# Two chained transformer blocks in one kernel: the experts' weight splits, the diff attention's order, an inverse's steps and the latent attention's meta keys

## The chip, the cores and the metric

The kernel runs on one core of one Trainium2 chip, as a single launch. The metric is device time in microseconds: the median of three runs. Beside it there is one profiled execution, with a time and a span of its own; every row below comes from that one. Engines are named as the profile names them: PE (TensorE matmuls) and PEld (its loads of the stationary operand), DVE (VectorE), ACT (ScalarE), POOL (GpSimd), SP (SyncE, here an issuer of DMAs).

## The reference

Two blocks run one after the other on x of 1024 tokens by 1024 columns, all in float32. The first has two layers, each of token mixers and an expert-choice FFN; layer 0 also carries 256 context tokens through both. The second is a gated delta rule layer and a latent attention layer. What the change touches:

```python
def diff_attn_core(q, k, v, lam):                    # 4 heads, two maps per head
    s = einsum('bqhmd,bkhmd->bhmqk', q, k) * (DIFF_D ** -0.5)
    a = softmax(s, axis=-1)
    w = a[:, :, 0] - lam * a[:, :, 1]
    return einsum('bhqk,bkhd->bqhd', w, v)

def expert_choice_ffn(x, router_w, wg, wu, wd):      # 16 experts, wg, wu, wd 1024x1024 each
    cap = 2 * n // 16                                # 128 tokens of x, 32 of the context
    aff = softmax(einsum('bnd,de->bne', x, router_w), axis=-1)
    gate, idx = top_k(aff.transpose(0, 2, 1), cap)
    xg = x[bidx, idx]
    hid = silu(einsum('becd,edf->becf', xg, wg)) * einsum('becd,edf->becf', xg, wu)
    o = einsum('becf,efd->becd', hid, wd) * gate[..., None]
    return zeros_like(x).at[bidx, idx].add(o)

def gated_delta_rule(q, k, v, g, beta):              # 8 heads, chunks of 64 tokens
    system = lower + eye(c)                          # lower: strictly lower triangle of kb k^T * decay
    sol = triangular_solve(system, rhs, left_side=True, lower=True)
    ...

def chunk_causal_attention(q, k, v):                 # 8 heads; 16 meta keys ahead of the 1024
    p = softmax(where(mask, q_blk k^T * scale, NEG), -1)
    return einsum('bhqk,bkhd->bqhd', p, v)
```

## The kernel before

The stages run in order: layer 0's mixers (diff attention 392 to 600 us of the span), its experts (about 949 to 1735), layer 1's mixers (diff attention 2055 to 2220), its experts (2505 to 3195), the delta layer (3195 to 4125, its heads 3300 to 3990), the latent layer's inputs, its attention (4490 to 4765) and its output (to the end). Float32 operands of large products are split into a high part (`wh`, written by ACT) and a low part (`wl`, what is left, by a subtraction), and each product is made of three matmuls: high by high, low by high, high by low. The instructions of an engine are put in order by a scheduler at build time that takes program order as the priority; semaphores between engines follow from the tiles.

**Experts.** `experts(l)` makes three products per expert, gate, up and down. `product` takes two halves of a weight; `weight` allots a raw tile of 2 MiB from the three buffers of `self.wr`, loads it on SP's queue, and splits it block by block: ACT copies 128x1024 to `wh` (L1165), DVE subtracts three of the four blocks, POOL the fourth (L1166). `wh` and `wl` have two buffers of four blocks. Each half then has 24 matmuls of 128x512 (L1187), and in layer 0, ahead of them, the context's: 16 matmuls with 32 stationary columns against the raw weight (L1181), which the trace shows as 32 records. `run` puts steps of other work between the yields of a product: the flips (`flip`: four transposes into the bank `t`, ACT's copy, DVE's subtraction L1134) and the hidden products. `fetch` gathers an expert's tokens and `scatter` adds its results, both through POOL (L1220).

**Diff attention.** `diff_unit` is one head by one block of 128 queries: 32 units in layer 1, 40 in layer 0 with the context's own 8. `a(m)` makes the scores of map m (PE, L591), their reduce (DVE, L592) and their exp (ACT, L594). `b` scales the second map by lambda and the ratio of the sums (DVE: reciprocal L598, one column L599, 128x1280 L600) and adds the two maps (POOL, L601). `c` transposes (L615) and copies (L616), `d` multiplies by V. `units` takes them in a pipeline: a(0) of unit k, b of unit k-1, a(1) of unit k, d of units k-3 and k-4, c of unit k-2.

**Inverses.** The triangular systems of a head are inverted by `inverse` for three groups of chunks: the meta tokens (`[8]`, one small chunk), and two groups of four. Each is a generator that yields after each set of small matmuls (64x64, 16 records a set) with an estimate of its cost. `inverses` takes one step of each in turn, and `weave` sets those steps between the matmuls of the next head's front (`zmul`, L1358).

**Latent attention.** `unit` in `latent_attend` is one head by one query block, 64 units. `a` makes scores and exp, `c` transposes the weights in blocks of 128 keys, the meta keys as a block of 16 (L2130), `d` multiplies by V: first the 16 meta rows (L2145), then the blocks (L2147).

Of the kernel before, what the change touches and what calls it, by code (L numbers as in the profile page):

```python
# [23 lines left out]
NE = 16  # L24
# [38 lines left out]
class Kernel:  # L63
# [490 lines left out]
    def units(self, q, new, steps):  # L554

        for i, u in enumerate(new):
            q.append(u)
            k = len(q) - 1
            old = [q[k - x] if k >= x else None for x in range(6)]
            if old[0]:  # L560
                old[0]["a"](0)
            if old[1]:
                old[1]["b"]()
            if old[0]:
                old[0]["a"](1)
            for x in (0, 1):
                if old[3 + x] and old[3 + x]["t"] % 2:
                    old[3 + x]["d"](old[4 + x], x)
            for x in (0, 1):
                if old[2]:  # L570
                    old[2]["c"](x)
            if old[0]:
                self.now = old[0]["sm"][:, 2:3]
            for _ in range(-(-len(steps) // (len(new) - i))):
                steps.pop(0)()

    def diff_unit(self, p, ps, V, Y, h, Z, t):
# [6 lines left out]
        def a(m):  # L584
# [7 lines left out]
            nc.vector.tensor_reduce(U["mx"][:, m:m + 1], S[:, :nk], AX.X, OP.min)  # L592
# [46 lines left out]
    def nbr_unit(self, p, ps, V, Y, h, H, i):  # L639
# [35 lines left out]
        def b():  # L675
# [434 lines left out]
    def experts(self, l):  # L1110
# [5 lines left out]
        with self.pool("ex") as p, self.banks("exps", m=3, c=1, t=1) as ps:  # L1116
# [52 lines left out]
            def product(U, key, x, name, e):  # L1169

                pm = U[key] = ps("m", 2)
                pc = None
                X = U[x]
                for half in range(2):
                    w, *W = weight(name, e, half)
                    if ctx and half == 0:
                        pc = U[key + "c"] = ps("c")
                    for k in range(4 if ctx else 0):
                        b = half * 4 + k
                        for g in range(4):  # L1180
                            nc.tensor.matmul(pc[g * 32:(g + 1) * 32, :256], U[x[0] + "cT"][:, b % 2 * 128 + b // 2 * 32:b % 2 * 128 + b // 2 * 32 + 32],  # L1181
                                             w[:, k, g * 256:(g + 1) * 256], start=b == 0, stop=b == 7)
                        yield
                    for k in range(4):
                        for q, (i, j) in enumerate(((0, 0), (0, 1), (1, 0))):
                            for c in range(2):
                                nc.tensor.matmul(pm[:, c], X[i][:, half * 4 + k], W[j][:, k, c * 512:(c + 1) * 512],  # L1187
                                                 start=half + k + q == 0, stop=half == 1 and k == 3 and q == 2)
# [44 lines left out]
            run(product(E[0], "g", "xT", "exp_w_gate", 0), [], 0)  # L1233
            silu(E[0])
            run(product(E[0], "u", "xT", "exp_w_up", 0), fetch(1), 0)
            for e in range(NE):
                U = E[e]
                steps = hidden(U)
                if e + 1 < NE:
                    run(product(E[e + 1], "g", "xT", "exp_w_gate", e + 1), steps, 1)  # L1240
# [4 lines left out]
                run(product(U, "d", "hT", "exp_w_down", e), [], 0)  # L1245
                scatter(U, e)
                if e + 1 < NE:
                    run(product(E[e + 1], "u", "xT", "exp_w_up", e + 1), fetch(e + 2) if e + 2 < NE else [], 0)
# [837 lines left out]
    def latent_attend(self, pw, p, ps, X):  # L2086
# [3 lines left out]

        def weight(c):
# [6 lines left out]
        def load(h):  # L2098
            H = {"mm": self.latent_head(X, h) if h else self.first}
            H["v"] = p.tile([128, 9, 128], F32, name="v", bufs=2)  # L2100
            hs = slice(h % 2 * 128, (h % 2 + 1) * 128)
            nc.sync.dma_start(H["v"][:, :8], self.vd[h // 2][16:, hs].rearrange("(t p) c -> p t c", p=128))
            nc.sync.dma_start(H["v"][:16, 8], self.vd[h // 2][:16, hs])
# [5 lines left out]
        def unit(H, h, i):  # L2109
# [15 lines left out]
            def c():  # L2125
                e = U["e"]
                eT = U["eT"] = p.tile([128, 9, 128], F32, name="eT", bufs=2)
# [213 lines left out]
```

## Time and profile before

| what | us |
|---|---|
| median of three runs (4869.22 to 4873.66) | 4869.98 |
| the profiled execution's own time | 4872.44 |
| its span | 4870.5 |

The span is what the profile's rows cover; 1.9 us of the profiled execution lie outside it. A window row gives the busy time of each engine in a stretch; the rest of the stretch is idle time of that engine. An engine at the full length of a stretch bounds it; where none is, waits between engines do.

### The profile page before, as it was taken

What the parts mean: (1) busy time and instruction counts of PE and PEld (TensorE: products, weight loads), DVE (VectorE), ACT (ScalarE), POOL (GpSimd) and SP (SyncE); (2) the same over time, 40 slices, a digit from 0 to 9 for tenths busy, and PEclk for the clock granted to TensorE, in tenths of its full rate; (3) what the DMA queues carried; (4) which work ended last, traced back from release to release, by engine and by line L of the source; (5) the groups of instructions that cost most, each with busy time, mean ns of one, the idle gap of its engine ahead of it and who ended that gap; (6) DMA issues with size and microseconds to landing.
All of it is one profiled execution on the core that took longest, in us unless ns stands there. A gap on an engine that the chain in (4) does not pass through costs nothing.

```text
span 4870.5 us, 77258 instructions
## 1 busy us (share of the span) xinstructions
PE 4427.4 (91%) x30151; PEld 3480.5 (71%) x30151; DVE 3183.5 (65%) x6512; ACT 2225.7 (46%) x4037; POOL 1358.2 (28%) x1033
## 2 busy tenths in 40 slices
PE   8998889799999979989959888879999998898899
PEld 4686676476777757867747666658888876787787
DVE  6536877755555566397778998856666663676551
ACT  3326653255555543376336656643333331454330
POOL 2214502244454422162124444412111100022111
PEclk9999899899999989999979999989999999999999
DMA  6422246687878722313548988821111123146757
GB/s 209 159 89 63 60 140 252 217 295 285 291 285 293 279 87 84 103 48 92 202 160 327 329 320 316 309 95 45 36 36 45 41 61 119 56 169 224 191 151 150
DMA packets 333997, 817.14 MB, mean 168 GB/s; under 512 B 32524, under 2 KB 125380, under 8 KB 333632
## 3 DMA queue, kind: packets, MB, share of 16 engines
q1 hardware_dynamic: 228368, 602.22, 34.2%
q0 software_dynamic: 51520, 125.07, 10.9%
q10 hardware_dynamic: 53744, 84.92, 5.0%
q8 instruction: 237, 3.88, 0.3%
q14 instruction: 128, 1.05, 0.1%
HBM read 690.47 MB, written 121.66 MB: 167 GB/s over the span
## 4 chain that ended last, share of the span: by engine, by line
PE 30%; DVE 8%; issue 5%; ACT 4%; DMA 3%; POOL 1%; SPq 0%; ACTq 0%; POOLq 0%; DVEq 0%
PE ps_z L1358 8%; PE ps_m L1187 5%; DVE wl L1166 4%; ACT wh L1165 2%; PE ps_mm L2211 2%; PE ps_S L2119 2%; PE ps_t L2147 1%; PE ps_m L917 1%; PE ps_i L1680 1%; PE ps_i L1694 1%; PE ps_m L1854 1%; PE ps_i L1687 1%; POOL wl L1166 1%; PE ps_t L1482 1%; PE ps_o L1599 1%
## 5 line engine op out<-in xcount | busy, mean ns | idle before, releaser
L1166 DVE TENSOR_TENSOR wl<-w,wh 128x1024 fp32r<-128x1024 f32 x576 | 843.5, 1508 | 179.7 <-ACT wh L1165 179.7
L1165 ACT ACTIVATE wh<-w 128x1024 fp32r<-128x1024 f32 x768 | 754.6, 1050 | 264.0 <-PE ps_m L1187 151.5
L1166 POOL TENSOR_TENSOR wl<-w,wh 128x1024 fp32r<-128x1024 f32 x192 | 535.7, 2825 | 634.9 <-ACT wh L1165 571.1
L1187 PE MATMUL ps_m<-wl,xTh 128*128 128x512 f32 x1024 | 344.6, 411 | 49.0 <-DVE wl L1166 33.6
L1187 PE MATMUL ps_m<-wh,xTh 128*128 128x512 f32 x1024 | 336.2, 410 | 1.4 <-ACT xTh L1133 1.4
L376 PE MATMUL ps_mm<-wh,hh 128*128 128x256 f32 (+1 forms) x928 | 322.5, 350 | 9.3 <-ACT wh L313 6.1
L1187 PE MATMUL ps_m<-wh,xTl 128*128 128x512 f32 x1024 | 325.1, 399 | 0.0
L376 PE MATMUL ps_mm<-wl,hh 128*128 128x256 f32 (+1 forms) x928 | 317.9, 344 | 2.7 <-DVE wl L314 2.6
L376 PE MATMUL ps_mm<-wh,hl 128*128 128x256 f32 (+1 forms) x928 | 316.1, 342 | 0.0
L1358 PE MATMUL ps_z<-hh,wh 128*128 128x350 f32 (+2 forms) x792 | 277.5, 351 | 2.0 <-ACT hh L1291 1.2
L1187 PEld LDWEIGHTS ps_m<-wl,xTh 128*128 128x128 f32 x1024 | 190.0, 192 | 114.4 <-DVE wl L1166 51.9
L1358 PE MATMUL ps_z<-hl,wh 128*128 128x350 f32 (+3 forms) x792 | 268.1, 339 | 0.0
L1358 PE MATMUL ps_z<-hh,wl 128*128 128x350 f32 (+2 forms) x792 | 264.5, 334 | 0.0
L601 POOL TENSOR_TENSOR e<-e,e 128x1280 f32<-128x1280 f32 (+1 forms) x72 | 191.6, 2661 | 188.2 <-DVE e L600 154.8
L1187 PEld LDWEIGHTS ps_m<-wh,xTh 128*128 128x128 f32 x1024 | 188.0, 192 | 64.2 <-issue 14.4
L1187 PEld LDWEIGHTS ps_m<-wh,xTl 128*128 128x128 f32 x1024 | 195.1, 192 | 41.3
L592 DVE TENSOR_REDUCE mx<-ps_S 128x1 f32<-128x1280 f32 (+1 forms) x144 | 196.1, 1366 | 37.0 <-PE ps_S L591 36.3
L376 PEld LDWEIGHTS ps_mm<-wh,hh 128*128 128x128 f32 x928 | 177.3, 192 | 48.0 <-issue 11.0
L376 PEld LDWEIGHTS ps_mm<-wl,hh 128*128 128x128 f32 x928 | 178.5, 192 | 22.4 <-DVE wl L314 4.4
L594 ACT ACTIVATE e<-ps_S,mx 128x1280 f32<-128x1280 f32 (+1 forms) x144 | 177.4, 1233 | 33.2 <-DVE mx L592 22.0
L376 PEld LDWEIGHTS ps_mm<-wh,hl 128*128 128x128 f32 x928 | 177.5, 192 | 18.8 <-issue 0.8
L1187 PE MATMUL ps_m<-wl,hTh 128*128 128x512 f32 x512 | 165.0, 403 | 20.5 <-DVE wl L1166 12.7
(661 smaller groups left out, 10754.0 us busy)
## 6 DMA issues: line engine op xcount, KB each, us to landing
w<-in_exp_w_gate SPq DMA_DIRECT2D x64, 2048.0 KB
w<-in_exp_w_up SPq DMA_DIRECT2D x64, 2048.0 KB
w<-in_exp_w_down SPq DMA_DIRECT2D x64, 2048.0 KB
w<-in_ada_w SPq DMA_DIRECT2D x12, 2048.0 KB
z<-zd POOLq DMA_DIRECT2D x76, 320.0 KB, 4.6
wraw<-in_ada_w SPq DMA_DIRECT2D x38, 512.0 KB
zd<-hi ACTq DMA_DIRECT2D x76, 256.0 KB
zw<-in_t_win SPq DMA_DIRECT2D x64, 256.0 KB
```

The source lines that it names most:

```text
L376: nc.tensor.matmul(pm[:, o:], hs[i][x][:, k, a * 128:(a + 1) * 128], w[:, k % 2, o:], start=q == 0, stop=q == 23)
L592: nc.vector.tensor_reduce(U["mx"][:, m:m + 1], S[:, :nk], AX.X, OP.min)
L594: nc.scalar.activation(e[:, :nk], S[:, :nk], AF.Exp, scale=-1.0, bias=U["mx"][:, m:m + 1], accum_out=U["sm"][:, m:m + 1])
L601: nc.gpsimd.tensor_add(w[:, :nk], w[:, :nk], U[0][:, :nk])
L917: nc.tensor.matmul(pm, a[:, k], b[:, k], start=k + x == 0, stop=k == 7 and x == 2)
L1165: nc.scalar.activation(wh[:, k], w[:, k], AF.Copy)
L1166: (nc.gpsimd if k == 3 else nc.vector).tensor_sub(wl[:, k], w[:, k], wh[:, k].bitcast(F32))
L1187: nc.tensor.matmul(pm[:, c], X[i][:, half * 4 + k], W[j][:, k, c * 512:(c + 1) * 512], start=half + k + q == 0, stop=half == 1 and k == 3 ...
L1358: nc.tensor.matmul(q[:M, :n], a[:, k % 4], b[:, k, z0:z0 + n], start=k == 0 and x == 0, stop=k == 7 and x == 2)
L1482: nc.tensor.transpose(pt[:r, i * 128:(i + 1) * 128], src[:, tok(t0 + i)[1]], self.ident)
L2119: nc.tensor.matmul(S[:, ks], q[:, i * 128:(i + 1) * 128], k[:, ks], start=x == 0, stop=x == 4)
L2211: nc.tensor.matmul(pm[:, c], a[:, k], b[:, k, c * 512:(c + 1) * 512], start=k + z == 0, stop=k == 7 and z == 2)
```

## The change

It has five parts. In `units`, both a(0) and a(1) of unit k come ahead of b of unit k-1, and b's L599 and L600 are put behind the second reduce of unit k on DVE. In `experts`, splitting becomes a queue: pieces of four blocks, one ahead, in layer 0; pieces of two blocks, three ahead, in layer 1, with `ahead + 1` and `ahead + 2` buffers; ACT's copies and the subtractions take two blocks per instruction, and all subtractions are DVE's. In layer 0 the context's matmuls of both halves stand at the start of a product. In layer 1 the context's bank of PSUM becomes a second one for the flips. `inverses` steps its two groups of four together, with one yield, and then the meta group. In `latent_attend` the meta keys are a block of 128: the transpose takes 128 columns, 16 rows are copied into a zeroed tile, and the product has 128 rows, 112 of them zero in both operands.

```diff
@@ units
             if old[0]:
                 old[0]["a"](0)
+                old[0]["a"](1)
             if old[1]:
-                old[1]["b"]()
-            if old[0]:
-                old[0]["a"](1)
+                old[1]["b"](old[0] and old[0].get("max"))
@@ diff_unit
-            nc.vector.tensor_reduce(U["mx"][:, m:m + 1], S[:, :nk], AX.X, OP.min)
+            U["max"] = nc.vector.tensor_reduce(U["mx"][:, m:m + 1], S[:, :nk], AX.X, OP.min).ins
...
-        def b():
+        def b(behind):
             sm, w = U["sm"], U[1]
             nc.vector.reciprocal(sm[:, 2:4], sm[:, 0:2])
-            nc.vector.scalar_tensor_tensor(sm[:, 3:4], sm[:, 3:4], self.nlam, sm[:, 0:1], op0=OP.mult, op1=OP.mult)
-            nc.vector.tensor_scalar(w[:, :nk], w[:, :nk], sm[:, 3:4], None, op0=OP.mult)
+
+            with self.tc.issue_after(behind) if behind else nullcontext():
+                nc.vector.scalar_tensor_tensor(sm[:, 3:4], sm[:, 3:4], self.nlam, sm[:, 0:1], op0=OP.mult, op1=OP.mult)
+                nc.vector.tensor_scalar(w[:, :nk], w[:, :nk], sm[:, 3:4], None, op0=OP.mult)
             nc.gpsimd.tensor_add(w[:, :nk], w[:, :nk], U[0][:, :nk])
@@ experts
-        with self.pool("ex") as p, self.banks("exps", m=3, c=1, t=1) as ps:
+        with self.pool("ex") as p, self.banks("exps", m=3, **(dict(c=1, t=1) if ctx else dict(t=2))) as ps:
...
-            def weight(name, e, half):
-                w = self.wr.tile([128, 4, 1024], F32, name="w", tag="w")
-                nc.sync.dma_start(w, A[name][l, e, half * 512:(half + 1) * 512].rearrange("(k p) f -> p k f", p=128))
-                wh, wl = [p.tile([128, 4, 1024], F32R, name=f"w{b}", bufs=2) for b in "hl"]
-                for k in range(4):
-                    nc.scalar.activation(wh[:, k], w[:, k], AF.Copy)
-                    (nc.gpsimd if k == 3 else nc.vector).tensor_sub(wl[:, k], w[:, k], wh[:, k].bitcast(F32))
-                return w, wh, wl
+            G, ahead = (4, 1) if ctx else (2, 3)
+            order = [("exp_w_gate", 0), ("exp_w_up", 0)]
+            for e in range(NE):
+                order += [("exp_w_gate", e + 1)] * (e + 1 < NE) + [("exp_w_down", e)] + [("exp_w_up", e + 1)] * (e + 1 < NE)
+            todo = [(name, e, k) for name, e in order for k in range(0, 8, G)]
+            ready = []
+
+            def split():
+
+                if not todo:
+                    return
+                name, e, k = todo.pop(0)
+                if k % 4 == 0:
+                    self.wraw = self.wr.tile([128, 4, 1024], F32, name="w", tag="w")
+                    nc.sync.dma_start(self.wraw, A[name][l, e, k * 128:(k + 4) * 128].rearrange("(k p) f -> p k f", p=128))
+                w = self.wraw[:, k % 4:k % 4 + G]
+                wh, wl = [p.tile([128, G, 1024], F32R, name=f"w{b}", bufs=ahead + (1 if ctx else 2)) for b in "hl"]
+                for i in range(0, G, 2):
+                    nc.scalar.activation(wh[:, i:i + 2], w[:, i:i + 2], AF.Copy)
+                    nc.vector.tensor_sub(wl[:, i:i + 2], w[:, i:i + 2], wh[:, i:i + 2].bitcast(F32))
+                ready.append((w, wh, wl))
+
+            def weight():
+                split()
+                return ready.pop(0)
+            for _ in range(ahead):
+                split()
...
-                for half in range(2):
-                    w, *W = weight(name, e, half)
-                    if ctx and half == 0:
+                for s in range(0, 8, G):
+                    w, *W = weight()
+                    if ctx and s == 0:
                         pc = U[key + "c"] = ps("c")
-                    for k in range(4 if ctx else 0):
-                        b = half * 4 + k
-                        for g in range(4):
...
-                        yield
-                    for k in range(4):
+
+                        for b in range(8):
+                            v = (w, ready[0][0])[b // 4]
+                            for g in range(4):
...
+                    for k in range(G):
+                        b = s + k
...
@@ inverses
-        runs = [self.inverse(p, ps, H, ts) for ts in ([8], [0, 1, 2, 3], [4, 5, 6, 7])]
-        while runs:
-            for g in list(runs):
-                c = next(g, None)
-                if c is None:
-                    runs.remove(g)
-                else:
-                    yield c
+        meta, *runs = [self.inverse(p, ps, H, ts) for ts in ([8], [0, 1, 2, 3], [4, 5, 6, 7])]
+
+        while None not in (steps := [next(g, None) for g in runs]):
+            yield sum(steps)
+            c = next(meta, None)
+            if c is not None:
+                yield c
@@ latent_attend
+        em, vm = [[p.tile([128, 128], F32, name=f"{x}m{i}") for i in range(3)] for x in "ev"]
+        for x in em + vm:
+            nc.gpsimd.memset(x, 0.0)
...
-            H["v"] = p.tile([128, 9, 128], F32, name="v", bufs=2)
+            H["v"] = p.tile([128, 8, 128], F32, name="v", bufs=2)
...
-            nc.sync.dma_start(H["v"][:16, 8], self.vd[h // 2][:16, hs])
+            nc.sync.dma_start(vm[h % 3][:16], self.vd[h // 2][:16, hs])
...
-                nc.tensor.transpose(pt[:16, 0:128], e[:, 0:16], self.ident)
+
+                nc.tensor.transpose(pt[:, 0:128], e[:, 0:128], self.ident)
...
-                self.copy(eT[:16, 8], pt[:16, 0:128])
+                x = U["em"] = em.pop(0)
+                em.append(x)
+                self.copy(x[:16], pt[:16, 0:128])
...
-                nc.tensor.matmul(po[:, :128], eT[:16, 8], v[:16, 8], start=True, stop=False)
+                nc.tensor.matmul(po[:, :128], U["em"], vm[h % 3], start=True, stop=False)
```

## Rows read from the trace of the kernel before

**Rows 1.** Windows: stretch, us, busy PE, PEld, DVE, ACT, POOL, clock, DMA share, GB/s.
```profile
1000.00:1680.00 680.00, 680.00 (x5035) 478.51 (x5029) 398.36 (x410) 389.71 (x453) 330.01 (x137) 1.00 0.80 287
2530.00:3112.00 582.00, 517.25 (x2225) 394.35 (x2224) 522.51 (x362) 364.25 (x406) 252.14 (x109) 0.98 0.88 322
2075.00:2215.00 140.00, 122.88 (x1002) 90.68 (x1001) 132.59 (x179) 111.40 (x194) 89.81 (x48) 0.99 0.19 47
3500.00:3600.00 100.00, 99.33 (x1043) 85.67 (x1042) 67.56 (x172) 35.69 (x87) 14.41 (x22) 1.00 0.13 44
4560.00:4760.00 200.00, 199.92 (x1357) 172.45 (x1356) 112.14 (x255) 78.05 (x190) 24.84 (x42) 1.00 0.67 168
```
**Rows 2.** Timeline of POOL, scatters of x: start, duration, instruction [idle before, releaser].
```profile
1024.11 2.30 POOL L1220 DMA_INDIRECT xd<-rd,idx  x1 [1.26 <-DVE rd L1219]
...
1698.15 2.28 POOL L1220 DMA_INDIRECT xd<-rd,idx  x1 [1.34 <-DVE rd L1219]
...
2608.81 2.40 POOL L1220 DMA_INDIRECT xd<-rd,idx  x1 [0.15 <-issue]
...
3159.19 2.29 POOL L1220 DMA_INDIRECT xd<-rd,idx  x1 [5.30 <-DVE rd L1219]
```
**Rows 3.** Timeline of PE's loads, one half of a product, layer 0.
```profile
1207.49 1.45 PEld L1181 LDWEIGHTS ps_c<-w,hcT 128*32 128x32 f32 x32 [0.35 <-issue]
1209.35 0.30 PEld L1187 LDWEIGHTS ps_m<-wh,hTh 128*128 128x128 f32 x2 [0.41 <-issue]
...
1215.01 1.02 PEld L1181 LDWEIGHTS ps_c<-w,xcT 128*32 128x32 f32 x24 [0.35 <-issue]
```
**Rows 4.** Groups by line, 1000 to 1680: count | busy us, mean ns | idle before.
```profile
L1166 DVE TENSOR_TENSOR wl<-w,wh 128x1024 fp32r<-128x1024 f32 x255 | 301.4, 1218 | 144.1 <-ACT wh L1165 144.1
```
**Rows 5.** The chain of waits from 2800 to 2870, its shares by line.
```profile
by line: DVE wl L1166 39.8%; PE ps_m L1187 26.1%; ACT wh L1165 12.7%; POOL wl L1166 6.8%; issue 6.2%; DVE rd L1219 3.7%; ACT ag L1196 2.7%; DVE xTl L1134 1.7%; ACT xTh L1133 1.4%; ACT hTh L1133 0.9%; PE ps_t L1131 0.6%; POOLq L1166 0.1%
```
**Rows 6.** Groups by line, 2530 to 3112 (layer 1).
```profile
L1166 DVE TENSOR_TENSOR wl<-w,wh 128x1024 fp32r<-128x1024 f32 x250 | 440.4, 1812 | 11.6 <-ACT wh L1165 11.6
```
**Rows 7.** Timeline of layer 1's experts, ACT, DVE and POOL.
```profile
2819.65 2.00 ACT L1165 ACTIVATE wh<-w 128x1024 fp32r<-128x1024 f32 x2
...
2820.65 14.62 DVE L1166 TENSOR_TENSOR wl<-w,wh 128x1024 fp32r<-128x1024 f32 x6
...
2821.06 5.26 POOL L1166 TENSOR_TENSOR wl<-w,wh 128x1024 fp32r<-128x1024 f32 x2
```
**Rows 8.** Groups by line, 2075 to 2215 (layer 1's diff attention).
```profile
L599 DVE SCALAR_TENSOR_TENSOR sm<-sm,nlam 128x1 f32<-128x1 f32 x28 | 24.1, 860 | 0.6
```
**Rows 9.** Timeline of layer 1's diff attention, DVE and POOL.
```profile
2125.84 0.21 DVE L599 SCALAR_TENSOR_TENSOR sm<-sm,nlam 128x1 f32<-128x1 f32 x1
...
2127.22 2.90 POOL L601 TENSOR_TENSOR e<-e,e 128x1280 f32<-128x1280 f32 x1 [1.97 <-DVE e L600]
...
2128.55 1.58 DVE L599 SCALAR_TENSOR_TENSOR sm<-sm,nlam 128x1 f32<-128x1 f32 x1
```
**Rows 10.** Timeline of PE in the delta heads.
```profile
3312.67 0.68 PE L1694 MATMUL ps_i<-TT,Xm 64*64 64x64 f32 x16
3313.28 0.43 PE L1358 MATMUL ps_z<-hh,wl 128*128 128x350 f32 x1
...
3603.23 1.15 PE L1687 MATMUL ps_i<-Tm,LT 64*64 64x64 f32 x32
3604.30 0.42 PE L1358 MATMUL ps_z<-hh,wh 128*128 128x350 f32 x1
...
3920.16 0.68 PE L1694 MATMUL ps_i<-TT,Xm 64*64 64x64 f32 x16
```
**Rows 11.** Timeline of PE in the latent attention, one unit's products.
```profile
4599.86 0.48 PE L2145 MATMUL ps_t<-v,eT 16*128 16x128 f32 x2
4600.28 1.60 PE L2147 MATMUL ps_t<-v,eT 128*128 128x128 f32 x12
4601.72 0.27 PE L2130 MATMUL ps_t<-ident,e 128*16 128x128 f32 x1
```

More of the change, by code (lines that the diff above doesn't have):

```diff
@@ L1 @@
 import math
-from contextlib import ExitStack, contextmanager
+from contextlib import ExitStack, contextmanager, nullcontext
 from itertools import chain
@@ L673, in a, with b @@
             nc.scalar.activation(e[:, n:n + 256], S[:, 768:], AF.Exp, bias=m, accum_out=sm[:, 2:3])
-        def b():
+        def b(behind):
             sm = U["sm"]
@@ L1169, in product @@
-            def product(U, key, x, name, e):
+            G, ahead = (4, 1) if ctx else (2, 3)
[17 more added lines that the diff above has]
+                ready.append((w, wh, wl))
@@ L1171, in product @@
+            def weight():
[3 more added lines that the diff above has]
+                split()
+            def product(U, key, x):
                 pm = U[key] = ps("m", 2)
-                pc = None
                 X = U[x]
-                for half in range(2):
-                    w, *W = weight(name, e, half)
-                    if ctx and half == 0:
+                for s in range(0, 8, G):
+                    w, *W = weight()
+                    if ctx and s == 0:
@@ L1177, in product @@
                         pc = U[key + "c"] = ps("c")
-                    for k in range(4 if ctx else 0):
-                        b = half * 4 + k
-                        for g in range(4):
-                            nc.tensor.matmul(pc[g * 32:(g + 1) * 32, :256], U[x[0] + "cT"][:, b % 2 * 128 + b // 2 * 32:b % 2 * 128 + b // 2 * 32 + 32],
-                                             w[:, k, g * 256:(g + 1) * 256], start=b == 0, stop=b == 7)
-                        yield
-                    for k in range(4):
+                        for b in range(8):
+                            v = (w, ready[0][0])[b // 4]
+                            for g in range(4):
+                                nc.tensor.matmul(pc[g * 32:(g + 1) * 32, :256], U[x[0] + "cT"][:, b % 2 * 128 + b // 2 * 32:b % 2 * 128 + b // 2 * 32 + 32],
+                                                 v[:, b % 4, g * 256:(g + 1) * 256], start=b == 0, stop=b == 7)
@@ L1185, in product @@
+                    for k in range(G):
+                        b = s + k
                         for q, (i, j) in enumerate(((0, 0), (0, 1), (1, 0))):
                             for c in range(2):
-                                nc.tensor.matmul(pm[:, c], X[i][:, half * 4 + k], W[j][:, k, c * 512:(c + 1) * 512],
-                                                 start=half + k + q == 0, stop=half == 1 and k == 3 and q == 2)
+                                nc.tensor.matmul(pm[:, c], X[i][:, b], W[j][:, k, c * 512:(c + 1) * 512],
+                                                 start=b + q == 0, stop=b == 7 and q == 2)
@@ L1232, in experts @@
                 f()
-            run(product(E[0], "g", "xT", "exp_w_gate", 0), [], 0)
+            run(product(E[0], "g", "xT"), [], 0)
             silu(E[0])
-            run(product(E[0], "u", "xT", "exp_w_up", 0), fetch(1), 0)
+            run(product(E[0], "u", "xT"), fetch(1), 0)
             for e in range(NE):
@@ L1239, in experts @@
                 if e + 1 < NE:
-                    run(product(E[e + 1], "g", "xT", "exp_w_gate", e + 1), steps, 1)
+                    run(product(E[e + 1], "g", "xT"), steps, 1)
                     silu(E[e + 1])
@@ L1244, in experts @@
                         f()
-                run(product(U, "d", "hT", "exp_w_down", e), [], 0)
+                run(product(U, "d", "hT"), [], 0)
                 scatter(U, e)
                 if e + 1 < NE:
-                    run(product(E[e + 1], "u", "xT", "exp_w_up", e + 1), fetch(e + 2) if e + 2 < NE else [], 0)
+                    run(product(E[e + 1], "u", "xT"), fetch(e + 2) if e + 2 < NE else [], 0)
     def h_src(self, t):
@@ L2126, in c @@
                 e = U["e"]
-                eT = U["eT"] = p.tile([128, 9, 128], F32, name="eT", bufs=2)
+                eT = U["eT"] = p.tile([128, 8, 128], F32, name="eT", bufs=2)
                 pt = ps("t")
                 n = min(3, i + 1)
-                nc.tensor.transpose(pt[:16, 0:128], e[:, 0:16], self.ident)
+                nc.tensor.transpose(pt[:, 0:128], e[:, 0:128], self.ident)
                 for j in range(n):
                     nc.tensor.transpose(pt[:, 128 + j * 128:256 + j * 128], e[:, 16 + j * 128:144 + j * 128], self.ident)
-                self.copy(eT[:16, 8], pt[:16, 0:128])
+                x = U["em"] = em.pop(0)
+                em.append(x)
+                self.copy(x[:16], pt[:16, 0:128])
                 self.copy(eT[:, :n].rearrange("p a b -> p (a b)"), pt[:, 128:128 + n * 128])
```

2 lines of the change are left out of this document (1 added, 1 removed).

## The prediction

> **What bounds the kernel now.** I read the stretches by stage first, because five different stages are edited and each has its own limit [rows 1]. The reader is to see which column fills each stretch. In the experts of layer 0 (1000 to 1680) PE is busy in every microsecond, so only PE's own instructions can be shortened there. In the experts of layer 1 (2530 to 3112) no column is full: DVE 522.51 of 582, PE 517.25, DMA share 0.88; several engines hand each other work. In the diff attention (2075 to 2215) DVE leads with 132.59 of 140. In the delta heads (3500 to 3600) and the latent attention (4560 to 4760) it is PE again, 99.33 of 100 and 199.92 of 200. [...] Next I read POOL's scatters, one per expert, for the period of an expert [rows 2]: 14 periods from 1024.11 to 1698.15 make 48.15 us in layer 0, 13 from 2608.81 to 3159.19 make 42.34 in layer 1. Then the groups of the splitting lines, the chain of waits and the timeline at the places of the edits.
>
> **Experts, layer 0.** PE is the limit, so what counts is what PE no longer does. Per half of a product (7.52 us, from 1207.49 to 1215.01) PE visits the context's 32-column matmuls once: 32 records, 1.45 us, with 0.35 of idle before them and 0.41 after [rows 3]. The matmuls stay, all 64 records of both halves in one visit; one visit per product loses its two sides. That saves 0.41 at least and 0.76 at most (an ordinary gap between two loads is part of both); I take 0.6. Three products by 16 experts are 48 visits: 48 x 0.6 = **-29** (-20 to -36).
>
> What covers the rest of the edit: POOL's quarter of the low parts goes to DVE. DVE outside the subtractions has 398.36 - 301.4 = 97 us in 14.1 experts, 6.9 each [rows 1, 4]; with all 24 blocks at 1.218 it would have 29.2 + 6.9 = 36.1 of 46.3 us, still under PE. By buffer: a pair is freed when PE ends a half, and the next but one half is split in the time of the half between. That is now either 5.44 (24 matmuls) and the 3.5 us visit, or the visit and 5.44: 8.9 either way. ACT's first two-block copy (about 2.0 us, what two blocks take now [rows 7]) and DVE's two subtractions (at most 2 x 2.44) end after 6.9, the first of them at 4.4. The context's visit wants both raw halves at the start of a product; the 16 DMA engines are busy 0.80 of 48.15 = 38.5 us per expert, which is 0.83 of the new period, so the loads still run ahead. If that cover goes, PE waits (rival D). The raw loads on SP's queue keep their number, size and three buffers; they move one half ahead, past no other load of that queue.
>
> **Experts, layer 1.** Here the chain of 2800 to 2870 is 39.8% DVE's subtraction, 12.7% ACT's copy, 6.8% POOL's subtraction and only 26.1% PE [rows 5]. The reason stands in the groups: DVE's 128x1024 subtraction means 1812 ns, against 1218 in layer 0 [rows 4, 6]. The timeline shows when it grows: from 2820.65 six of them took 14.62 us while POOL did two (5.26 us from 2821.06) [rows 7]; without POOL they would take 6 x 1.218 = 7.3, and the difference, 7.3, is more than POOL's 5.26. DVE stands still while POOL subtracts. The change takes POOL out of it, gives five buffers of two blocks for two of four, and runs three ahead.
>
> The period cannot fall below the longest engine. DMA: 0.88 x 42.34 = 37.3. DVE: (522.51 - 440.4) / 13.75 experts = 6.0, with 24 x 1.218 = 35.2 together. PE: 6 x 5.44 = 32.7 and its flips, about 35. ACT: 364.25 / 13.75 = 26.5. With three pieces ahead PE has 3 x 2.72 = 8.2 us of work when a piece begins its 4.4 us of copy and subtraction, so it no longer waits for each one; what remains is that loads bunch behind three raw buffers. Between the floor (37.3: -80 over 16 experts) and a period set by bunched loads as now (41.8: -8) I take 39.3, nearer the floor since the trace puts the waits on the splits and not on loads: 16 x 3.0 (42.34 - 39.3) = **-48**. The PSUM bank of the context goes to a second flip bank, priced at nothing: flips are 4 x 4 short transposes per expert, and the bank can only free them.
>
> **Diff attention.** A unit takes 140/28 = 5.0 us of a stretch in which DVE has 132.59 [rows 1, 8]. Its one-column L599 means 860 ns [rows 8]; at 2128.55 it took 1.58 while POOL's 2.90 us add (from 2127.22) ran, at 2125.84, with POOL free, 0.21 [rows 9]. The difference of the mean, 0.65, is a standstill. Putting L599 and L600 behind the second reduce of the next unit moves them past the preceding add: at most 32 x 0.65 = 21 in layer 1; in layer 0 an estimate of 19, for 40 units of which 8 are context alone. What is late next: PE has 122.88/28 = 4.39 per unit and ACT 3.98, so the floor behind DVE's 4.35 is near. And L601 starts later by about one reduce; the transposes of that unit wait for it. L599 now waits for that reduce, but both are DVE's and in its order; queued behind it are evictions of earlier units, for which PE's pair products are not due before. I take half, **-20** (-40 to +19).
>
> **Inverses in lockstep.** PE-bound, so again the visits count. A lone visit of 16 records costs 0.61 until the next product's matmul (3312.67 to 3313.28), a paired one of 32 costs 1.07 (3603.23 to 3604.30) [rows 10]: two lone ones joined save 2 x 0.61 - 1.07 = 0.15. Visits of one chunk group stand 91 times between 3300 and 3990 (63 alone, from the row at 3312.67 to that at 3920.16, and 28 with two small records of the meta group beside them), against 75 of both groups. 45 pairs by 0.15 are **-7**, the most there is; half of it if half of them meet anyway. The other way, a step has one slot less of other work between it and its eviction: if a third of the 91 then waited the 0.15 that it saves now, +5.
>
> **Padded keys.** The two records with 16 rows take 0.42 (4599.86 to 4600.28); twelve with 128 rows take 1.44 to the next transpose at 4601.72, 0.12 each [rows 11]. Padded to 128 rows the pair would take 0.24: 64 units by 0.18 are -12, and with the two changes of tile size around it up to -19. I take **-14**. The transpose grows from 16 to 128 columns beside three neighbours of 128, and the copy keeps its 16 rows. Six memsets on POOL, which has 24.84 of 200 there, are hidden; alone they are under 2 us. The 16-row load on SP stays one per head.
>
> [...]
>
> **Sum.** -29 - 48 - 20 - 7 - 14 = -118. The profiled execution took 4872.4 (span 4870.5 and 1.9 around it), 2.5 over the median; 4872.4 - 118 - 2.5 = **4752**.
>
> **Rivals.**
> A. Layer 1 stays paced by its loads. For it: DMA share 0.88, the fullest of any stretch [rows 1]. Against it: the chain names splits. -8 for -48: 4792.
> B. The reorder of diff attention backfires: the later add holds the transposes by 0.9 (a reduce of 1.48 less the 0.6 it no longer loses), and PE at 4.39 of 5.0 has little to hide it. Of the 0.9, 0.6 is the stretch that went; 72 units (32 and 40) by 0.27 net are +19 for -20: 4791.
> C. Lockstep and padding buy nothing: what the 16-row pair costs over 0.24 is a change of PE's state that comes with the next product anyway, and the joined visits find their sides again. For it: each figure rests on one place of its view. +3 for each (the slots lost; 64 transposes longer by a few hundredths) for -21: 4779.
> D. Layer 0 loses its cover: DVE takes over 4 us more than now per half, and PE waits. 48 products by 2 us are +96 for -29: 4877, no change.
> E. The other sign: DVE's stretch in layer 1 comes not from POOL but from the loads' traffic, and stays at 1.812 with 24 blocks: 43.5 + 6.0 = 49.5 per expert, +7.1 by 16 = +114 for -48: 4914. The stage gains nothing from 1.51 us a block (24 x 1.51 + 6.0 = 42.3), the whole is even at 1.70, where the other terms' 70 are gone. Against it, layer 0 moves 287 GB/s with no stretch [rows 1, 4].
> F. Layer 1 reaches its floor and diff attention gains in full: 4752 - 32 - 20 = 4700.
>
> **Chances.** Forecast 0.43 (its own range 4728 to 4776), A 0.18, B 0.09, C 0.10, F 0.10, D 0.04, E 0.06. The range goes from 4695 to 4805: it holds all but D, E and the ends. What this kernel's measurement can tell from no change is about 0.2%, 10 us. Faster: all but D and E, 0.90; same 0.04 (D); slower 0.06 (E).
>
> **What would show it.** Scatters 46.3 apart in layer 0 with PE still full, and 64 small records in one visit; 39 apart in layer 1 with DVE's 2048-wide subtraction at 2.3 to 2.45 and no POOL row on that line; L599 near 0.21 everywhere and units 4.7 apart; no lone 16-record visits of the inverse; no 16-row matmul in latent attention. Wrong it would be by a DVE subtraction over 2.9, by PE idle on raw loads at the start of a product, or by transposes of the diff units waiting for L601.

## The result and the profile after

The changed kernel takes 4716.28 us (median of 4, 4707.3 to 4724.71) against 4870.88 (median of 4): a ratio of 0.9682, 95% interval 0.9663 to 0.9700, 154.6 us less. The prediction was 4752, 118 less; the direction was right and the time is in its range (4695 to 4805), though below the narrower range of the forecast itself (4728 to 4776). The profiled execution of the changed kernel has a span of 4722.9, 147.6 less than the one before.

To see where it came from, each stage is measured on PE, from its first to its last matmul as the groups by line give them: scores to last transpose for the diff attention, the large products for the experts, the heads' products (`zmul`) for the delta layer, first score to the output's first matmul for the latent attention.

| stage (us) | before | after | difference | predicted |
|---|---|---|---|---|
| diff attention, layer 0 | 207.3 | 199.9 | -7.4 | -20, both layers together |
| experts, layer 0 | 774.8 | 753.7 | -21.1 | -29 |
| diff attention, layer 1 | 174.0 | 166.4 | -7.6 | see layer 0 |
| experts, layer 1 | 677.9 | 588.0 | -89.9 | -48 |
| delta heads (inverses) | 773.5 | 766.7 | -6.8 | -7 |
| latent attention | 275.2 | 264.2 | -11.0 | -14 |
| sum | | | -143.8 | -118 |

Another 3.8 lies between the stages. In other profiled runs of the unchanged parts these lengths come back within 3 us, layer 0's diff attention within 5.

The windows of the kernel after, with the columns of [rows 1]:

```profile
980.00:1680.00 700.00, 700.00 (x5334) 516.63 (x5333) 509.27 (x345) 395.39 (x300) 127.71 (x56) 1.00 0.82 295
2500.00:3030.00 530.00, 514.78 (x2351) 418.38 (x2350) 475.87 (x293) 366.15 (x248) 71.59 (x26) 1.00 1.00 372
2050.00:2180.00 130.00, 119.32 (x1004) 89.70 (x1005) 116.36 (x179) 108.65 (x189) 90.54 (x49) 1.00 0.22 51
3400.00:3500.00 100.00, 99.78 (x1080) 87.29 (x1076) 64.13 (x165) 35.86 (x88) 12.89 (x18) 1.00 0.11 39
4425.00:4615.00 190.00, 186.39 (x1368) 171.66 (x1367) 113.68 (x259) 78.49 (x192) 24.84 (x42) 1.00 0.71 178
```

Two rows changed their kind. In layer 1's experts (second row) the DMA share went from 0.88 to 1.00 and the rate from 322 to 372 GB/s, and PE from 0.89 of the stretch to 0.97. In the diff attention (third row) DVE no longer leads: 116.36 of 130 beside PE's 119.32, where it had 132.59 of 140. POOL's scatters give the periods, as in [rows 2]:

```profile
1016.91 3.37 POOL L1242 DMA_INDIRECT xd<-rd,idx  x1 [7.56 <-DVE rd L1241]
...
1671.04 3.35 POOL L1242 DMA_INDIRECT xd<-rd,idx  x1 [7.62 <-DVE rd L1241]
...
2559.99 3.39 POOL L1242 DMA_INDIRECT xd<-rd,idx  x1 [26.78 <-DVE rd L1241]
...
3032.22 1.56 POOL L1242 DMA_INDIRECT xd<-rd,idx  x1 [33.26 <-DVE rd L1241]
```

That is 14 periods of 46.72 in layer 0 (48.15 before, 46.3 forecast) and 13 of 36.33 in layer 1 (42.34 before, 39.3 forecast). The second is under 37.3, which the prediction called a floor. The groups and waits of layer 1 show the stretch of [rows 6] gone (2 x 1143 ns an instruction) and what is late next, ACT's copy waiting for the weights:

```profile
L1182 DVE TENSOR_TENSOR wl<-w,wh 128x2048 fp32r<-128x2048 f32 x176 | 394.1, 2285 | 50.5 <-ACT wh L1181 50.3
L1181 ACT ACTIVATE wh<-w 128x2048 fp32r<-128x2048 f32 x175 | 325.9, 1912 | 134.3 <-DMA w<-in_exp_w_gate 67.9 <-DMA w<-in_exp_w_up 48.2 <-DMA w<-in_exp_w_down 14.4
```

### The profile page after: what moved, and what is told of

It reads as the page before. It is cut to its first block, busy times and chain, and to the rows that moved or that the text cites. A ratio compares the mean times of both kernels' runs of the same rounds, so it can differ in the third digit from the quotient of the medians.

```text
span 4722.9 us, 76062 instructions
## 1 busy us (share of the span) xinstructions
PE 4332.3 (92%) x30151; PEld 3477.6 (74%) x30151; DVE 3179.9 (67%) x6320; ACT 2188.3 (46%) x3653; POOL 903.1 (19%) x847
## 4 chain that ended last, share of the span: by engine, by line
PE 26%; DMA 8%; DVE 8%; issue 5%; ACT 2%; POOL 1%; SPq 0%; ACTq 0%; POOLq 0%; DVEq 0%
PE ps_z L1380 9%; DVE wl L1182 4%; DMA w<-in_exp_w_gate 2%; PE ps_mm L2240 2%; PE ps_S L2145 2%; PE ps_m L1209 1%; DMA w<-in_exp_w_down 1%; PE ps_m L918 1%; PE ps_t L2176 1%; PE ps_i L1715 1%; PE ps_i L1708 1%; DMA w<-in_exp_w_up 1%; PE ps_m L1875 1%; PE ps_i L1701 1%; DMA w<-in_b_w_out 1%
## 5 line engine op out<-in xcount | busy, mean ns | idle before, releaser
L1182 DVE TENSOR_TENSOR wl<-w,wh 128x2048 fp32r<-128x2048 f32 x384 | 862.4, 2286 | 211.1 <-ACT wh L1181 208.8
L1181 ACT ACTIVATE wh<-w 128x2048 fp32r<-128x2048 f32 x384 | 717.5, 1910 | 322.3 <-PE ps_m L1209 174.9
L1209 PE MATMUL ps_m<-wl,xTh 128*128 128x512 f32 x1024 | 324.7, 396 | 9.5 <-DVE wl L1182 9.3
L1209 PEld LDWEIGHTS ps_m<-wh,xTl 128*128 128x128 f32 x1024 | 191.5, 188 | 46.3 <-issue 6.2
L1242 POOL DMA_INDIRECT xd<-rd,idx x32 | 104.7, 3271 | 421.6 <-DVE rd L1241 383.6
```

Of the source, the lines that this page charges most:

```text
L1181: nc.scalar.activation(wh[:, i:i + 2], w[:, i:i + 2], AF.Copy)
L1182: nc.vector.tensor_sub(wl[:, i:i + 2], w[:, i:i + 2], wh[:, i:i + 2].bitcast(F32))
L1209: nc.tensor.matmul(pm[:, c], X[i][:, b], W[j][:, k, c * 512:(c + 1) * 512], start=b + q == 0, stop=b == 7 and q == 2)
L1242: nc.gpsimd.indirect_dma_start(out=dst, out_offset=bass.IndirectOffsetOnAxis(ap=idx[:, e:e + 1], axis=0), in_=r, in_offset=None, compute_o ...
```

## Experiments: layer 1's experts

Each run below is given with its median time in us, its ratio to the kernel before as measured beside it (95% interval in brackets), and the length of its stage, taken as in the table above. The stage is what the runs are compared by.

Two theories. P: DVE stands still while POOL subtracts, and that is most of what the stage lost. Q: the queue counts, that is the deeper run-ahead in smaller pieces.

**POOL's quarter alone moved**, in the kernel before.

```diff
-(nc.gpsimd if k == 3 else nc.vector).tensor_sub(wl[:, k], ...)
+(nc.gpsimd if ctx and k == 3 else nc.vector).tensor_sub(wl[:, k], ...)
```

> The kernel before, with layer 1's fourth block subtracted on DVE like the other three, and nothing else changed. Layer 1's experts last 678 us before and 588 after the change, from their first to their last large matmul. Theory P (DVE stands still while POOL subtracts, and that is most of the stage's loss): DVE's 128x1024 subtraction falls from 1812 to about 1218 ns, DVE needs some 35 us per expert, the stage ends near 620 or below, and the whole near 4815. Theory Q (the queue is what counts: two buffers of four blocks let PE wait for each split): the subtraction falls too, but the stage stays above 650 and the whole above 4840.

Measured: 4775.78, ratio 0.9817 (0.9800 to 0.9834); the stage takes 595.3. One edit of a few words brings 82.6 of the 89.9, more than P had expected (620 or below). Its group, window row and DMA rate:

```profile
L1166 DVE TENSOR_TENSOR wl<-w,wh 128x1024 fp32r<-128x1024 f32 x329 | 382.1, 1216 | 29.6 <-ACT wh L1165 29.6
...
2530.00:3040.00 510.00, 492.69 (x2206) 390.19 (x2205) 459.72 (x440) 362.77 (x400) 40.88 (x26) 0.99 0.99 365
```

The subtraction is back at 1216 ns, as in layer 0 [rows 4], and the DMA share is already 0.99.

**POOL's quarter put back** into the changed kernel, its queue kept.

```diff
+if ctx or k % 4 == 0:
     nc.vector.tensor_sub(wl[:, i:i + 2], ...)
+else:
+    for j, eng in ((0, nc.vector), (1, nc.gpsimd)):
+        eng.tensor_sub(wl[:, j], w[:, j], wh[:, j].bitcast(F32))
```

> The changed kernel, with layer 1's fourth block back on POOL (one 128x1024 subtraction of every four blocks), its queue of five buffers and three pieces ahead kept. Theory P: DVE's subtractions stretch again, the stage goes from 588 back to 640 or more, the whole to some 4770 or more. Theory Q: the run-ahead hides the stretch, the stage stays below 610, the whole below 4740.

Measured: 4766.27, ratio 0.9799 (0.9782 to 0.9816); the stage takes 637.6, between the two forecasts and close to P's 640. P holds for the cause: two timelines (POOL's, then DVE's) show one DVE subtraction of 2.28 stretched to 7.32 over POOL's work, which goes on to 2811.5:

```profile
2806.17 5.32 POOL L1186 TENSOR_TENSOR wl<-w,wh 128x1024 fp32r<-128x1024 f32 x2
...
2806.33 7.32 DVE L1183 TENSOR_TENSOR wl<-w,wh 128x2048 fp32r<-128x2048 f32 x1
```

Q has a part here: with the stall in place, the changed kernel's other edits (queue, wide instructions, flip bank, not separated in this run) bring the stage from 677.9 to 637.6.

**The short queue** (pieces of four blocks, one ahead, two buffers) in the changed kernel, without POOL's subtraction.

```diff
-G, ahead = (4, 1) if ctx else (2, 3)
+G, ahead = 4, 1
...
-... bufs=ahead + (1 if ctx else 2)
+... bufs=ahead + 1
```

> The changed kernel, with layer 1 in pieces of four blocks, one ahead, in two buffers, as layer 0 has them; all subtractions on DVE, two blocks an instruction. Theory P: the stage stays below 615, the whole below 4745. Theory Q: the stage goes back above 640, the whole above 4765.

Measured: 4719.25, ratio 0.9704 (0.9687 to 0.9720); the stage takes 588.5 against 588.0. Q falls: once POOL is out, the deeper queue of pieces is worth nothing.

**One flip bank** in place of two.

```diff
-self.banks("exps", m=3, **(dict(c=1, t=1) if ctx else dict(t=2)))
+self.banks("exps", m=3, c=1, t=1)
```

> The changed kernel, with one PSUM bank for the flips of layer 1 in place of two. The prediction priced the second bank at nothing: the stage stays at 588 within 3 us. The rival, that flips wait for ACT and DVE to clear the one bank and so hold PE: 64 flips by some 0.5 us, 32 us more.

Measured: 4725.03, ratio 0.9710 (0.9691 to 0.9729); the stage takes 593.2, so the bank is worth about 5, not nothing and far from 32. The run of POOL's quarter alone (595.3) lacks 7.3 against the change; that the bank is most of it there too was not run.

## Experiments: diff attention

**No order edge**: a(0), a(1), b in the new order of the program, nothing forced on DVE.

```diff
-old[1]["b"](old[0] and old[0].get("max"))
+old[1]["b"](None)
```

> The changed kernel without the order that puts L600 and L601 (L599 and L600 before) behind the next unit's second reduce; a(0), a(1), b stay in the new order of the program. Layer 1's diff attention lasts 174 us before and 166 after, from its first score matmul to its last transpose. If the forced order is what keeps the one-column multiplication out of POOL's add, that instruction goes back from 274 to some 800 ns and the stage to 172 or more; if the order of the program is enough, both stay, 166 within 2.

Measured: 4736.96, ratio 0.9731 (0.9715 to 0.9747). Layer 1's stage takes 175.3, layer 0's 210.3: without the edge nothing of the gain is left. In layer 1 the one-column instruction goes back to a mean of 532 ns, part of the way only, because it meets the add at some places and not at others. The timelines of POOL and DVE where it does:

```profile
2106.47 2.91 POOL L602 TENSOR_TENSOR e<-e,e 128x1280 f32<-128x1280 f32 x1 [2.79 <-DVE e L601]
...
2106.22 1.48 DVE L591 TENSOR_REDUCE mx<-ps_S 128x1 f32<-128x1280 f32 x1
2107.62 0.15 DVE L597 RECIPROCAL sm<-sm 128x2 f32<-128x2 f32 x1
2107.80 1.59 DVE L600 SCALAR_TENSOR_TENSOR sm<-sm,nlam 128x1 f32<-128x1 f32 x1
```

The reduce, which reads PSUM, and the reciprocal take 1.48 and 0.15 beside the same add, as they do elsewhere; the one-column instruction takes 1.59. With the edge, over the same stage of the changed kernel, it is 0.27 ([rows 8] had 860 ns):

```profile
L600 DVE SCALAR_TENSOR_TENSOR sm<-sm,nlam 128x1 f32<-128x1 f32 x28 | 7.7, 274 | 0.2
```

The step from 532 to 274, 32 times, is 8.3 us, about what the edge is worth in layer 1 (8.9). But the new order of the program alone took it from 860 to 532, and the stage got no shorter for it (175.3 against 174.0): DVE's idle time on the scores rose from 4.3 us in 140 to 11.0 in 130. So a shorter standstill is not enough by itself, and that the edge's gain goes through it is argued from its size.

**No add on POOL** (the sum of the two maps is left out).

```diff
-nc.gpsimd.tensor_add(w[:, :nk], w[:, :nk], U[0][:, :nk])
```

> The changed kernel without POOL's add in the diff attention, so that only the second map, scaled, goes on to the transposes: what is left out is the sum of the two maps. If PE, ACT and DVE are now the limit of a unit (the prediction's reason for taking half of the stall), the stage stays at 166 within 4. If the add still holds units up (its start behind the reduce, its 2.9 us, DVE's wait on it), the stage falls below 155.

Measured: 4711.35, ratio 0.9679 (0.9663 to 0.9695). Layer 1's stage takes 163.8 for 166.4: there the add is nearly free, and the other engines are the limit. Layer 0's takes 184.4 for 199.9: there it still costs 15.5. The first expectation holds for layer 1, of which it spoke; layer 0's loss was not foreseen. The groups of layer 0's stage before (392 to 600), after the change (393 to 593) and in this run (393 to 577) show where it comes from:

```profile
L599 DVE SCALAR_TENSOR_TENSOR sm<-sm,nlam 128x1 f32<-128x1 f32 x40 | 24.8, 621 | 0.5
...
L600 DVE SCALAR_TENSOR_TENSOR sm<-sm,nlam 128x1 f32<-128x1 f32 x40 | 22.5, 562 | 0.3
...
L600 DVE SCALAR_TENSOR_TENSOR sm<-sm,nlam 128x1 f32<-128x1 f32 x40 | 8.5, 212 | 0.5
```

In layer 0 the edge left the standstill nearly as it was (621 to 562 ns). Without the add it is gone, and 40 x 0.35 = 14.0 is most of the 15.5. What layer 0's 7.4 us came from is therefore open. The mean granted clock of its stage, as a share of full speed, differs too: 0.88 before, 0.90 after, 0.85 without the edge, 0.94 here, and 0.84 in a run whose diff attention is the change's own (visits apart, below), where the stage took 204.3. How much of layer 0's differences goes with the clock was not separated.

## Experiments: latent attention

**Narrow transpose**, 16 columns, with the product on 128 rows.

```diff
-nc.tensor.transpose(pt[:, 0:128], e[:, 0:128], self.ident)
+nc.tensor.transpose(pt[:16, 0:128], e[:, 0:16], self.ident)
```

> The changed kernel with the meta keys' transpose back at 16 columns, the product still on 128 rows. Latent attention lasts 264.2 us from its first score matmul to the output's first matmul (275.2 before). [...] By the rows (0.11 from the 16-column transpose to the next, and 0.11 from the 128-column one) nothing changes, or it is longer where tile sizes alternate: 264 to 268.

Measured: 4713.89, ratio 0.9683 (0.9662 to 0.9705); the stage takes 262.7 for 264.2, within its spread. The transpose's columns cost nothing that can be told from it.

**Narrow product**, 16 rows, with the transpose on 128 columns.

```diff
-nc.tensor.matmul(po[:, :128], U["em"], vm[h % 3], ...)
+nc.tensor.matmul(po[:, :128], U["em"][:16], vm[h % 3][:16], ...)
```

> The changed kernel with the meta keys' product back on 16 rows, the transpose still on 128 columns. If the rows of the product are what costs, the pair takes 0.42 again in place of 0.30 and latent attention goes from 264.2 to about 272 to 275. If loads go by columns alone, it stays at 264.

Measured: 4734.49, ratio 0.9725 (0.9709 to 0.9741); the stage takes 278.9, 14.7 more and a little past the 272 to 275 expected: the product's rows are the whole gain. PE's timeline of the changed kernel, and of this one:

```profile
4463.39 0.43 PE L2174 MATMUL ps_t<-vm,em 128*128 128x128 f32 x2
4463.65 1.50 PE L2176 MATMUL ps_t<-v,eT 128*128 128x128 f32 x12
4464.99 0.27 PE L2157 MATMUL ps_t<-ident,e 128*128 128x128 f32 x1
```

```profile
4461.03 0.48 PE L2174 MATMUL ps_t<-vm,em 16*128 16x128 f32 x2
4461.44 1.60 PE L2176 MATMUL ps_t<-v,eT 128*128 128x128 f32 x12
4462.89 0.27 PE L2157 MATMUL ps_t<-ident,e 128*128 128x128 f32 x1
```

The pair takes 0.26 against 0.41, and the twelve behind it 1.34 against 1.45: the 16-row product costs on itself and again on the 128-row one after it. 0.15 + 0.11 is 0.26 a unit at this place; the stage's mean is 14.7 / 64 = 0.23. The product in front pays as well: over the 45 units in which the pair is followed directly by its blocks, the pair takes 0.30 against 0.42 on average, and the step from the record ahead of it to the pair 0.12 against 0.21.

## Experiments: layer 0's experts, and three edits more

**Visits apart**: each half's context matmuls ahead of that half again.

```diff
-if ctx and s == 0:
-    pc = U[key + "c"] = ps("c")
-    for b in range(8):
-        v = (w, ready[0][0])[b // 4]
+if ctx:
+    if s == 0:
+        pc = U[key + "c"] = ps("c")
+    for b in range(s, s + 4):
+        v = w
```

> The changed kernel with the context's matmuls in two visits per product again, each ahead of its half; everything else of the change is kept, POOL's quarter on DVE and the two-block instructions too. Layer 0's experts last 774.8 us before and 753.7 after, from their first to their last large matmul. If the joined visit is all that changed there, the stage goes back to 775 within 2. If the move of POOL's quarter or the wide instructions had their part, it stops between 758 and 770; if the move had cost something that the joined visit covers, it goes above 778.

Measured: 4741.03, ratio 0.9743 (0.9727 to 0.9759); the stage takes 769.3. So joining the visits brings 15.6 (0.33 a product), and other edits bring 5.5. The loads of the joined visit in the changed kernel, as in [rows 3]:

```profile
1201.20 3.18 PEld L1203 LDWEIGHTS ps_c<-w,xcT 128*32 128x32 f32 x64 [0.35 <-issue]
1204.79 0.30 PEld L1209 LDWEIGHTS ps_m<-wh,xTh 128*128 128x128 f32 x2 [0.41 <-issue]
```

The 64 records take 3.18, more than twice the 1.45 of 32. That takes 0.28 from the 0.6 for the side that went and leaves 0.32, close to the 0.33 of the run. The single records of the trace show why. They start in groups of four: the first two groups of a visit together, each later one some 0.216 after the last. So 32 records more are eight steps more, 8 x 0.216 = 1.73, which is 3.18 - 1.45. A record is no dearer in the long visit; a visit that starts anew has a cheaper start and end, and 1.45 is not the price of 32 records more.

**POOL's quarter kept in layer 0**, visits joined.

```diff
+if not ctx or i == 0:
     nc.vector.tensor_sub(wl[:, i:i + 2], ...)
+else:
+    for j, eng in ((2, nc.vector), (3, nc.gpsimd)):
+        eng.tensor_sub(wl[:, j], w[:, j], wh[:, j].bitcast(F32))
```

> The changed kernel with POOL's quarter of the subtractions kept in layer 0 (the joined visit of the context's matmuls stays). Layer 0's experts take 753.7 us after the change. With visits apart they took 769.3, and before 774.8, so 5.5 us of the gain are not the visit's. If POOL's leaving made them, the stage goes to 758 to 760 here; if the two-block instructions and the order of the queue made them, it stays at 754 within 2.

Measured: 4733.0, ratio 0.9718 (0.9703 to 0.9733); the stage takes 762.7, 9.0 more, and a little past the 758 to 760 expected. The groups of this run, from 1000 to 1680, show the same standstill, now in layer 0:

```profile
L1186 DVE TENSOR_TENSOR wl<-w,wh 128x1024 fp32r<-128x1024 f32 x87 | 230.5, 2649 | 0.0
```

The kernel before did not have it: there POOL's quarter stood in layer 0 as well, and DVE's mean was 1218 [rows 4]. DVE was mostly done with its blocks and waiting for ACT, 144.1 us idle of the 680. In this run ACT's copy of two blocks releases DVE's third block and POOL's fourth at once, and PE, full before and after, is busy in 675.68 of 680. So the 9.0 are what POOL's quarter costs beside the two-block copies. That its leaving made the 5.5 us is not shown; they stay open.

**A fourth raw buffer, the add in two parts, and the meta group's step joined**, together.

```diff
+own = not ctx and len(todo) // 2 % 4 == 0
-self.wraw = self.wr.tile([128, 4, 1024], F32, name="w", tag="w")
+self.wraw = p.tile([128, 4, 1024], F32, name="w4", bufs=1) if own else self.wr.tile(...)
-G, ahead = (4, 1) if ctx else (2, 3)
+G, ahead = (4, 1) if ctx else (2, 2)
...
-nc.gpsimd.tensor_add(w[:, :nk], w[:, :nk], U[0][:, :nk])
+for x in (slice(0, 512), slice(512, nk)) if nk > 512 else (slice(0, nk),):
+    nc.gpsimd.tensor_add(w[:, x], w[:, x], U[0][:, x])
...
-yield sum(steps)
-c = next(meta, None)
-if c is not None:
-    yield c
+yield sum(steps) + next(meta, 0.0)
```

> The changed kernel with three more edits, each in a stage of its own. One: layer 1's experts with a fourth raw buffer of 2 MiB (and two pieces ahead in place of three, to make room). The DMA engines are full there after the change, and nearly idle ahead of the stage, so a load more ahead of it is worth 2 MiB at 372 GB/s, 5.6 us of 588; if PE or DVE is the limit, nothing. Two: POOL's add in the diff attention in two parts, 512 columns and the rest, so that the first transposes can begin sooner. Without any add layer 0 took 184.4 us for 199.9 and layer 1 163.8 for 166.4; half of that, 8 and 1, if the transposes' wait for it is the cost; nothing or a loss of 2 to 5 if it is DVE's standstill under POOL. Three: the meta group's step of the inverse in the same yield as the two others. If each visit has a fixed side of 0.15, 62 visits fewer are 9 us of 766.7; by the rows after (0.14 for a lone visit of two records, 1.08 for 32, 1.22 for both) nothing.

Measured: 4692.42, ratio 0.9647 (0.9631 to 0.9664). Layer 1's experts take 559.8, 28 less, five times what was expected of one load more ahead (that two pieces ahead do as well as three is inferred from the run of the short queue). The diff attention takes 192.9 and 163.9, 7.0 and 2.5 less: the transposes' wait is part of the cost. The delta heads take 775.9, 9 more, which nobody expected: PE now waits for DVE before a head's products, in a view of its waits (us in total, times, longest) that had no such line before:

```profile
PEld ps_z L1382 <- DVE c L1462: 6.5, 6, 1.1
PE ps_z L1382 <- DVE c L1462: 4.8, 6, 0.8
```

That is 5 of the 9; the rest was not found.

**Without the third edit**: the fourth buffer and the divided add.

> The changed kernel with the fourth raw buffer and the add in two parts, and the inverse's steps as the change has them. The run with all three edits took 559.8 in layer 1's experts, 192.9 and 163.9 in the diff attention and 775.9 in the delta heads; if the edits do not touch each other's stages, the delta heads return to 766.5 and the rest stays: about 4683 to 4685.

Measured: 4678.5 (median of 5), ratio 0.9611 (0.9598 to 0.9625), the fastest kernel of this study, 38 under the change. The delta heads are back at 766.9, layer 1's experts stay at 560.0, the diff attention takes 190.3 and 164.6. Window and scatters of layer 1's experts in this kernel:

```profile
2500.00:3000.00 500.00, 499.75 (x2312) 413.62 (x2311) 469.82 (x288) 367.06 (x245) 71.63 (x27) 1.00 1.02 390
```

```profile
2618.56 3.40 POOL L1244 DMA_INDIRECT xd<-rd,idx  x1 [11.80 <-DVE rd L1243]
...
2929.41 9.98 POOL L1244 DMA_INDIRECT xd<-rd,idx  x1 [31.14 <-DVE rd L1243]
```

Nine periods of 34.54: ACT's waits for the weights, 137.5 us in the changed kernel from 2475 to 3063, are gone from this run's waits (2460 to 3022), and what ACT waits for is PE, 54.3. PE is full, and the DMA engines, whose share was already 1.00, move 390 GB/s in place of 372. The share said that they were busy, not that they could do no more.

## Why the prediction was right, and which sizes were off

The time fell into the range because the mechanism of layer 1's experts was right. How far off it was is partly luck: that stage brought 42 more than its term, and the terms of layer 0's experts, of the diff attention and of the padded keys fell short by 16 together.

**Experts, layer 1**: the mechanism was right (DVE stands still while POOL subtracts: P, shown from both sides), the size was not, -48 for -89.9. The term that was mis-sized is the period of 39.3. The larger part of the miss is the 2.0 that it kept above the floor for bunched loads: 16 x 2.0 = 32. The rest is the floor itself, "DMA: 0.88 x 42.34 = 37.3", too high by 1.0: 16 us. (By periods that is 48; the whole stage came out 42 shorter than forecast.) The bytes of an expert are fixed, the time that the engines are busy with them is not: the kernel after needs 36.33, the last experiment 34.54, close to the PE floor ("about 35") of the same paragraph. The second reason given there, three pieces ahead, was wrong: the short queue does as well. Bunched loads behind three raw buffers, named as what would remain, did remain, but cost 36.33 - 34.54 = 1.8 a period over PE's own; a fourth buffer removed them. The bank priced at nothing is worth 5. Rivals A and E are refuted by the run of POOL's quarter alone.

The runs show the standstill: 2.28 became 7.32 beside 5.32 of POOL, a one-column instruction took 1.59 and not 0.21, and the reduce, which reads PSUM, stays at 1.48 beside the add. What in the chip makes DVE wait was not shown.

**Experts, layer 0**: -29 for -21.1. The term for the visits was too large, 0.6 a product where 0.33 was measured: it set only an ordinary gap against the two sides that go, and the joined visit is also 0.28 longer than two short ones. Other edits bring 5.5, which the prediction did not have; which of them is open. Rival D, the lost cover, did not come: PE is busy in 700.00 of 700.

**Diff attention**: -20 for -15. The standstill is there, and without the edge nothing of the gain is left. Layer 1 went much as described: the one-column instruction is at 274 ns, and of the 21 at most 7.6 were gained, with PE and ACT close behind; even no add at all brings only 2.6 more. In layer 0 the step "moves them past the preceding add" failed: 562 ns, not the 0.21 that was to be seen everywhere. There the add still costs 15.5, and dividing it gave back 7 to 10. That layer 0 gained 7.4 all the same has no shown cause.

**Inverses**: -7 for -6.8, but not by the count that was forecast. In PE's timeline the visits of one chunk group (16 records, or 18 with two of the meta group) fall from 93 (3300 to 3990, 91 by the prediction's count) to 35 (3172 to 3856): 29 pairs in place of 45, 4.4 us by 0.15 each. 21 lone visits of 16 records remain, where the prediction said none. The other 2.4 are within the spread of the stage, and no run isolates this edit, so the agreement is in part luck.

**Padded keys**: -14 for -11.0, and 14.7 by the run that undoes the product's rows alone. The pair itself saved 0.12, not the 0.18 of the sum; the neighbours, which the prediction named as the two changes of tile size, made up for a part. Rival C's half, that the padding buys nothing, did not come. The loads alone would have said it: in the trace before (medians, 4480 to 4800) the product's load of 16 rows takes 0.184 beside 0.192 for 128, and the transpose's load of 16 columns 0.093 beside 0.140 for its neighbours of 128, 64 x 0.047 = 3.0 us. But 16 columns or 128 in the transpose are the same within the spread of the stage, and 16 rows or 128 in the product are 0.23 a unit apart. What the rows here show is the spacing of whole products when the tile size changes, 0.41 against 0.26 for the pair.

## What to carry to other kernels

An instruction on a second engine that is meant to relieve DVE can stop it, as a subtraction here went from 2.28 to 7.32 us beside 5.32 of POOL: look for a DVE instruction whose mean has grown, and try the work on DVE alone before building deeper queues. The same split can be harmless where the two do not meet, as in layer 0 before the change (a mean of 1218 ns against 1812 in layer 1), so read it stage by stage. A busy share times a period is no floor when the engine's rate still rises (here from 372 to 390 GB/s at a share of 1.00 and 1.02); work out the floor from bytes and the best rate seen, and try one more buffer in flight even at a share of 1.00. A small product with few rows between full ones can be priced by its neighbours too (here 0.11 on the twelve products behind it, beside 0.15 on its own), so read the spacing from the instruction ahead of it to the second one behind it.

## What the hardware showed that was not expected

With the DMA engines' share at 1.00, a fourth 2 MiB buffer (with two pieces ahead in place of three) raised the rate from 372 to 390 GB/s and took 28 us out of 588. The 390 are a mean over 500 us. And 64 small records in one visit took 3.18 us, where two visits of 32 took 2 x 1.45: the records of a visit come in groups of four, the first two together and each later one some 0.216 after the last.
